# Summing the MLP's quarter products: additions by VectorE into SBUF, or accumulating DMAs into DRAM

## The chip, the cores and the metric

The kernel runs on one core of a Trainium2 chip. The metric is the device time of one execution in microseconds (us). Before the change the median of three runs is 1222.51 us.

The engines are named as the profile names them: PE is TensorE (matmuls; PEld are its weight loads), DVE is VectorE, ACT is ScalarE, POOL is GpSimd, SP is SyncE, which issues nearly all DMAs. SBUF is the on-chip memory of 128 partitions, PSUM the eight banks that matmuls write, DRAM the memory outside the core.

## The reference

One layer of a decoder trunk, for a prompt of 1024 tokens and a sample group of 8 x 8 tokens, in fp32, with a width of 1024. The change touches the MLP at the end of the layer alone:

```python
    h2 = rms_norm(x, norm2_g[l]) * (1.0 + scale2[:, None]) + shift2[:, None]
    ff = jnp.square(jax.nn.relu(h2 @ w_ff1[l])) @ w_ff2[l]
    x = x + gate2[:, None] * ff
```

`w_ff1` is 1024 x 4096 and `w_ff2` is 4096 x 1024. What comes before it (adaptive norm, one input projection, retention, windowed attention, two convolution modules, the output projection, a gated residual) gives `x`, the kernel's `x1`.

## The kernel before

All activations are held feature-major: 128 partitions by 8 feature blocks by 1088 tokens (1024 of the prompt and 64 of the sample). Every fp32 operand of a matmul is split into two parts, `hi` and `lo` (ACT rounds a copy, DVE subtracts it), and each product is three matmuls: hi by hi, hi by lo, lo by hi.

The MLP runs over 4096 hidden features in 8 groups (`NG`) of 4 blocks (`G`) of 128. For each group, `ff1_block` makes the hidden block from `h2`, for three chunks of tokens (384, 384 and 320 wide, `CH`), and `ff1_out` evicts it by ACT as Relu and Square. For `w_ff2`, a group's product is a product of 2 x 2 matrices of quarters: the group's weights and its hidden features are cut into quarters, and instead of eight quarter products seven are made, from sums and differences of quarters (Strassen's scheme in Winograd's form). The results go to four quarters of the output, named (i, j): i is the half of the 1024 output features (x1's blocks 4i to 4i + 3), j the half of the 1024 prompt tokens (512 columns, `H`).

The loop over g = 0 to 6 does one group's seven products, each in one call of `slot`, and between them the ff1 blocks of the next group (`ff1_items`, one or two blocks between two slots). In `slot`, for each of four output blocks m, `products` issues six matmuls of 128x512 into a PSUM bank (seven banks turn), and `add_to` adds the bank to every quarter of `x1` that needs it, by DVE; some products go to two quarters, so there are 40 such additions a group. The first group writes instead of adding. Quarter (1, 1) of `x1`, called `s22`, at the same time holds the sum that three of the four output quarters share. `x1` itself has been copied to DRAM before (`save`, `x1_save` in the profile, line 1407), so that its place is free for the sums.

The sample's 64 tokens go another way: `sample_parts` makes `st` (one ACT cast, one DVE subtraction), `sample_product` makes matmuls with it into a bank `sm`, and `sample_out` adds these into `acc`.

The eighth group is done in the plain way, four by four products with `products` over both halves of the features, 16 banks in the order (i, t) = (0, 0), (0, 1), (1, 0), (1, 1), four each. With it the output is finished: the old x1 is loaded from DRAM as `xr`, DVE adds `s22` to the two quarters that need it, then for every bank forms gate * sum + xr in place and adds gate * bank, and SP stores the result (line 1619).

PE, ACT and DVE keep the order of the program from `pinned[0] = True` on. The DMAs are not pinned: their order on a queue is chosen by the scheduler of the framework, by the times at which it takes them to be ready. Waits are put in by the framework from the overlaps of what is read and written, in SBUF and DRAM alike. `form` and `two` split an operand into its parts, `quarter` loads a quarter of `w_ff2` in SP's queue (line 1328), `loaded_weight` an ff1 block (line 1293).

All operations that go through the wrapper `InOrder` (ACT and DVE) carry its line in the profile, L158, and all matmuls L171; they are told apart by the names of their tiles.

Of the kernel before, what the change touches and what calls it, by code (L numbers as in the profile page):

```python
# [8 lines left out]
F32 = mybir.dt.float32  # L9
F32R = mybir.dt.float32r  # L10
AF = mybir.ActivationFunctionType
ALU = mybir.AluOpType
# [3 lines left out]
P = 128  # L16
D = 1024
NT = 1088
SEQ = 1024
# [121 lines left out]
def decoder_step(ctx: ExitStack, tc: tile.TileContext, A, O, where):  # L141
    nc = tc.nc
# [21 lines left out]
    ACT, DVE = InOrder(nc.scalar), InOrder(nc.vector)  # L164
# [44 lines left out]
    first = lambda n: view(cfirst, "cfirst", n)  # L209
# [119 lines left out]
    with ExitStack() as gctx:  # L329
# [765 lines left out]
        x = M[:, :, SEQ:]  # L1095
# [18 lines left out]
        def slot(c, i, evac, functions=None):  # L1114
            c0, w = CH[c]
            ps = mm_psum(w)
            product(ps, *ready[i], act_of(h, c), range(8))
            if i >= 4 or c == 2:
                tick()
            if functions:  # L1120
                table(functions)
            evac(IN_BLOCKS[i], c, c0, w, ps)
# [67 lines left out]
        for c, (c0, w) in enumerate(CH):  # L1190
            for j in range(2):
                ps = mm_psum(w)
# [9 lines left out]
            for j in range(2):  # L1202
                o, g = M[:, MA + j, c0 : c0 + w], gate[j][:, c0 : c0 + w]
# [7 lines left out]
    with ExitStack() as fctx:  # L1211
        xp = fctx.enter_context(tc.tile_pool(name="xp", bufs=1))
        x1 = xp.tile([P, 8, NT], F32, tag="x1", name="x1")
# [102 lines left out]

        NG = FF // P // G
        H = 512  # L1320
        RAW = ("w", "w", "ar", "ar")
# [73 lines left out]
        for c in range(3):  # L1395
            for b in range(G) if c < 2 else (2, 3, 0, 1):
                ps = mm_psum(CH[c][1])
# [10 lines left out]
                if c == 2 and b == 3:  # L1408
                    now_parts = two(a11, "ah", "al"), two(u.quarter(0, 0), "qh", "ql")
# [12 lines left out]
            parts = room(side + "h", F32R), room(side + "l", F32R)  # L1422
            return parts, cast(raw, *parts)

        def add_to(g, x, ps):

            i, j, m, minus, first = x
            dst = x1[:, 4 * i + m, H * j : H * j + H]
            if first and g == 0:
                if minus:  # L1430
                    DVE.tensor_scalar_mul(dst, ps, -1.0)
                else:
                    DVE.tensor_copy(dst, ps)
            else:
                DVE.tensor_tensor(out=dst, in0=dst, in1=ps, op=ALU.subtract if minus else ALU.add)

        def sample_parts(g, u):

# [30 lines left out]
        t = first_sum(u)  # L1469

        for g in range(NG - 1):
            nu = Group()
            state = {"f": 0}

            def ff1_items(n):
                for _ in range(n):
                    f = state["f"]
                    state["f"] += 1
                    b, c = f // 3, f % 3
                    x = G * (g + 1) + b  # L1480
                    ps = next_bank()[:, : CH[c][1]]
                    ff1_block(nu, x, c, ps)
                    ff1_out(nu, x, c, ps)
                    if c == 0:
                        ff1_split(x + 1)
                        ff1_load(x + 2)

            def slot(parts, targets, rests):

                rests = list(rests)  # L1490
                for m in range(4):
                    ps = next_bank()
                    products(ps, m, *parts, True, True)
                    if rests:
                        rests.pop(0)()
                    for i, j, minus, first in targets:
                        add_to(g, (i, j, m, minus, first), ps)


            DVE.tensor_tensor(out=s, in0=s, in1=a22, op=add)  # L1500
            w, r0 = form(s, "a")
            v, r1 = form(t, "q")
            parts2 = (w, v)
            slot(now_parts, [(0, 0, 0, 1), (1, 1, 0, 1)], [r0, r1])
            st = sample_parts(g, u)
            ff1_items(1)
            sm = sample_bank()
            sample_product(sm, st, now_parts[0], 0, True, False)
            ff1_items(1)


            DVE.tensor_tensor(out=s, in0=s, in1=a11, op=sub)
            DVE.tensor_tensor(out=t, in0=u.quarter(1, 1), in1=t, op=sub)
            w, r0 = form(s, "a")
            v, r1 = form(t, "q")
            parts3 = (w, v)
            slot(parts2, [(1, 1, 0, 0), (1, 0, 1, 1)], [r0, r1])
            a11 = quarter(g, 0, 0)
            ff1_items(2)


            DVE.tensor_tensor(out=t, in0=u.quarter(1, 0), in1=t, op=sub)
            w, r0 = form(a12, "a")
            v, r1 = form(u.quarter(1, 0), "q")
            parts4 = (w, v)
            slot(parts3, [(1, 1, 0, 0)], [r0, r1])
            ff1_items(2)


            t3 = u.quarter(0, 1)  # L1530
            DVE.tensor_tensor(out=t3, in0=u.quarter(1, 1), in1=t3, op=sub)
            DVE.tensor_tensor(out=s, in0=a12, in1=s, op=sub)
            w, r0 = form(s, "a")
            v, r1 = form(u.quarter(1, 1), "q")
            parts5 = (w, v)
            slot(parts4, [(0, 0, 0, 0)], [r0, r1])
            a21, a22 = quarter(g, 1, 0), quarter(g, 1, 1)
            sample_product(sm, st, parts4[0], 1, False, True)
            sample_out(g, 0, sm)
            ff1_items(1)  # L1540


            DVE.tensor_tensor(out=a11, in0=a11, in1=a21, op=sub)
            w, r0 = form(a11, "a")
            v, r1 = form(t3, "q")
            parts6 = (w, v)
            slot(parts5, [(0, 1, 0, 1)], [r0, r1])
            nxt = quarter(g + 1, 0, 0)
            ff1_items(2)


            w, r0 = form(a22, "a")
            v, r1 = form(t, "q")
            parts7 = (w, v)
            slot(parts6, [(1, 1, 0, 0), (0, 1, 1, 0)], [r0, r1])
            last = g + 1 == NG - 1
            s = quarter(g + 1, 0 if last else 1, 1 if last else 0)
            ff1_items(1)


            w, r0 = form(a21, "a")
            slot(parts7, [(1, 0, 0, 0)], [r0])
            sm = sample_bank()
            sample_product(sm, st, parts7[0], 1, True, False)
            sample_product(sm, st, w, 0, False, True)
            sample_out(g, 1, sm)
            if not last:
                a11 = nxt
                now_parts = two(a11, "ah", "al"), two(nu.quarter(0, 0), "qh", "ql")
                t = first_sum(nu)  # L1570
                a22, a12 = quarter(g + 1, 1, 1), quarter(g + 1, 0, 1)
                ff1_items(2)
            else:
                weights, parts = {(0, 0): two(nxt, "ah", "al")}, {(0, 0): two(nu.quarter(0, 0), "qh", "ql")}
                weights[0, 1] = two(s, "wh", "wl")
                ff1_items(1)
                parts[1, 0] = two(nu.quarter(1, 0), "q12", "t")
                ff1_items(1)
            u = nu


        g = NG - 1
        raw = [quarter(g, 1, j) for j in range(2)]
        xr = [hp.tile([P, 4, CH[0][1]], F32, tag=("hi0", "lo0", "hi1", "lo1")[m % 4], name=nm("xr")) for m in range(8)]
        xr = [x.rearrange("p a b -> p (a b)")[:, 0:SEQ] for x in xr]
        for m in range(8):
            nc.sync.dma_start(xr[m], save[:, m, :])
        s22 = x1[:, 4:8, H:SEQ]

        def sample_end(i):  # L1590

# [10 lines left out]
        for i in range(2):  # L1602
            for t in range(2):
                for m in range(4):
                    ps = next_bank()
                    for j in range(2):
                        products(ps, m, weights[i, j], parts[j, t], j == 0, j == 1)
                    if i == t == m == 0:
                        parts[0, 1] = two(u.quarter(0, 1), "qh", "ql")
                        parts[1, 1] = two(u.quarter(1, 1), "fr", "q11")  # L1610
                        st = sample_parts(g, u)
                    if (t, m) == (i, 0) and i == 0 or (t, m) == (1, 3) and i == 0:
                        x = x1[:, 0:4, H:SEQ] if m == 0 else x1[:, 4:8, 0:H]
                        DVE.tensor_tensor(out=x, in0=x, in1=s22, op=ALU.add)
                    x = x1[:, 4 * i + m, H * t : H * t + H]
                    gate = mod[:, 40 + 4 * i + m, 0:1]
                    DVE.scalar_tensor_tensor(x, x, gate, xr[4 * i + m][:, H * t : H * t + H], ALU.mult, ALU.add)
                    DVE.scalar_tensor_tensor(x, ps, gate, x, ALU.mult, ALU.add)
                    nc.sync.dma_start(O["yT"][:, 4 * i + m, H * t : H * t + H], x)
                    if i == 0 and t == 0 and m >= 2:  # L1620
                        weights[1, m - 2] = two(raw[m - 2], "ah", "al") if m == 3 else two(raw[0], "wh", "wl")
                    if t == 0 and m == 3:
                        sm = sample_bank()
                        for j in range(2):
                            sample_product(sm, st, weights[i, j], j, j == 0, j == 1)
                        sample_out(g, i, sm)
                    if t == 1 and m == 1:
                        sample_end(i)
# [74 lines left out]
```

## Time and profile before

| | |
|---|---|
| runs | 1222.51 us median, 1221.91 to 1224.81 |
| the profiled execution | 1222.88 us, its span 1220.8 us |
| granted TensorE clock | 0.999 |
| busy, share of the span | PE 99%, PEld 90%, DVE 66%, ACT 38%, POOL 1% |
| DMA | 113.72 MB, mean 93 GB/s |
| MLP loop, one group | 89.94 us |

A row of a timeline gives the start and the duration in us, the engine, the line, the operation, out<-in, and in square brackets how long the engine had been idle and what ended it. A row of a group gives the count, busy us, the mean in ns, and after the bar the idle time before. A row of waits gives who waited for whom: us in total, times, the longest. A row of DMA issues gives the queue's engine, the count, the size of one, and the median us from issue to landing. SPq is SP's queue.

### The profile page before, as it was taken

The numbers are of one execution on the slowest core, as the hardware profiler recorded it, in microseconds if no ns is written. First come the engines' busy times: TensorE is split into PE (matmuls) and PEld (weight loads), VectorE is DVE, ScalarE is ACT, GpSimd is POOL, SyncE is SP. The second block draws the span as 40 slices with busy tenths as digits, with TensorE's granted clock in tenths as the row PEclk, the third lists the DMA queues.
The fourth block names the chain that finished last, engine by engine and source line by source line (L and its number), as shares of the span: only waits on it lengthen the run. The fifth ranks groups of instructions, "written<-read, shape, count | busy, mean of one in ns | idle before, by whom it ended". The sixth has DMA issues, their size and how long they took to land.

```text
span 1220.8 us, 17251 instructions
## 1 busy us (share of the span) xinstructions
PE 1206.5 (99%) x7054; PEld 1095.5 (90%) x7054; DVE 809.7 (66%) x1288; ACT 465.0 (38%) x941; POOL 8.2 (1%) x28
## 2 busy tenths in 40 slices
PE   8999999999999999999999999999999999999998
PEld 6897789988899999989999999999999999999887
DVE  4789798884697538646566666666566566566575
ACT  4452333432367325633333334233333333333330
POOL 0000000000000000000000000000000000000000
PEclk9999999999999999999999999999999999999999
DMA  9748711120120813111211211221221121121332
GB/s 344 267 163 300 211 36 36 52 55 19 36 72 23 283 53 134 36 35 54 85 52 70 69 54 68 70 69 53 69 85 53 53 86 52 56 83 52 121 125 91
DMA packets 60165, 113.72 MB, mean 93 GB/s; under 512 B 13495, under 2 KB 29623, under 8 KB 60087
## 3 DMA queue, kind: packets, MB, share of 16 engines
q1 hardware_dynamic: 59943, 112.56, 27.9%
q8 instruction: 55, 0.90, 0.3%
q14 instruction: 23, 0.19, 0.1%
q10 hardware_dynamic: 144, 0.07, 0.0%
HBM read 101.90 MB, written 10.72 MB: 92 GB/s over the span
## 4 chain that ended last, share of the span: by engine, by line
PE 87%; DVE 8%; ACT 2%; SPq 1%; DMA 1%; issue 1%; DVEq 0%; ACTq 0%
PE ps L171 47%; PE mm L171 29%; PE pm L171 6%; DVE x L158 3%; PE sm L171 3%; PE pm L175 1%; PE ada L171 1%; DMA M<-in_xT 1%; SPq L391 1%; DVE al L158 1%; ACT ah L158 1%; DVE ql L158 1%; ACT q L158 0%; DVE qh L305 0%; DVE lo L312 0%
## 5 line engine op out<-in xcount | busy, mean ns | idle before, releaser
L171 PE MATMUL ps<-hi,wl 128*128 128x384 f32 (+1 forms) x672 | 219.9, 327 | 0.0
L171 PE MATMUL ps<-hi,wh 128*128 128x384 f32 (+1 forms) x672 | 219.7, 327 | 0.0
L171 PE MATMUL ps<-lo,wh 128*128 128x384 f32 (+1 forms) x672 | 219.4, 326 | 0.0
L171 PE MATMUL mm<-hi,wh 128*128 128x384 f32 (+1 forms) x544 | 181.8, 334 | 0.4 <-ACT hi L158 0.4
L171 PE MATMUL mm<-lo,wh 128*128 128x384 f32 (+1 forms) x544 | 178.0, 327 | 0.5 <-DVE lo L158 0.4
L171 PE MATMUL mm<-hi,wl 128*128 128x384 f32 (+1 forms) x544 | 177.5, 327 | 0.5 <-DVE wl L158 0.5
L158 ACT ACTIVATE q<-ps 128x384 f32<-128x384 f32 (+1 forms) x112 | 42.5, 380 | 351.8 <-PE ps L171 351.8
L158 DVE TENSOR_TENSOR x<-x,ps 128x512 f32<-128x512 f32 x264 | 165.3, 681 | 0.4 <-PE ps L171 0.4
L171 PE MATMUL ps<-qh,al 128*128 128x512 f32 x408 | 159.8, 392 | 0.0
L171 PE MATMUL ps<-qh,ah 128*128 128x512 f32 x408 | 159.2, 390 | 0.6 <-ACT us L1386 0.6
L171 PE MATMUL ps<-ql,ah 128*128 128x512 f32 x408 | 159.6, 391 | 0.0
L171 PEld LDWEIGHTS ps<-hi,wh 128*128 128x128 f32 x672 | 126.3, 188 | 2.2
L171 PEld LDWEIGHTS ps<-lo,wh 128*128 128x128 f32 x672 | 126.2, 188 | 2.2
L171 PEld LDWEIGHTS ps<-hi,wl 128*128 128x128 f32 x672 | 126.2, 188 | 0.0
L171 PEld LDWEIGHTS mm<-hi,wh 128*128 128x128 f32 x544 | 102.2, 188 | 8.9 <-issue 6.4
L171 PEld LDWEIGHTS mm<-lo,wh 128*128 128x128 f32 x544 | 102.3, 188 | 1.4 <-DVE lo L158 1.4
L171 PEld LDWEIGHTS mm<-hi,wl 128*128 128x128 f32 x544 | 102.1, 188 | 1.0 <-DVE wl L158 1.0
L158 DVE TENSOR_TENSOR wl<-fr,wh 128x1024 fp32r<-128x1024 f32 x27 | 33.1, 1226 | 102.4 <-ACT wh L158 102.4
L614 DVE SCALAR_TENSOR_TENSOR M<-glu,cmix,M 128x512 f32<-128x512 f32 (+2 forms) x150 | 97.8, 667 | 2.0
L171 PEld LDWEIGHTS ps<-qh,al 128*128 128x128 f32 x408 | 76.6, 188 | 16.1
L171 PEld LDWEIGHTS ps<-qh,ah 128*128 128x128 f32 x408 | 76.7, 188 | 15.4 <-ACT us L1386 0.9
L171 PEld LDWEIGHTS ps<-ql,ah 128*128 128x128 f32 x408 | 76.6, 188 | 14.7
(346 smaller groups left out, 1822.0 us busy)
## 6 DMA issues: line engine op xcount, KB each, us to landing
w<-in_w_ff SPq DMA_DIRECT2D x29, 512.0 KB, 3.6
ar<-in_w_ff SPq DMA_DIRECT2D x28, 512.0 KB, 3.7
fr<-in_w_ff SPq DMA_DIRECT2D x28, 512.0 KB, 3.6
w<-in_w_in SPq DMA_DIRECT2D x22, 512.0 KB, 5.0
M<-in_ada SPq DMA_DIRECT2D x20, 512.0 KB, 4.8
ada<-in_ada SPq DMA_DIRECT2D x16, 512.0 KB, 10.5
sw<-in_ada SPq DMA_DIRECT2D x9, 512.0 KB, 5.3
w<-in_w_out SPq DMA_DIRECT2D x8, 512.0 KB, 3.4
```

The lines of the kernel that those rows point to most:

```text
L158: i = f(*args, **kw)
L171: return tc.keep_in_program_order(nc.tensor.matmul(*args, **kw))
L175: return tc.keep_in_program_order(nc.tensor.transpose(*args, **kw))
L391: nc.sync.dma_start(t.rearrange("p (a k) -> p a k", a=4), src)
L614: DVE.scalar_tensor_tensor(dst, src(t), cdw[:, j, t : t + 1], dst, ALU.mult, ALU.add))))
```

## The change

The additions into `x1` by DVE are taken out of the loop. In their place ACT copies each bank of products out of PSUM into a stage, and two banks (one pair, 512 KB) are sent from POOL's queue by DMA into `kept`, a DRAM tensor with six sums: a plain DMA where a sum is written for the first time, an accumulating one (`accum_op=ALU.add`) afterwards. The stages are three of `x1`'s feature blocks (5, 6 and 7, their 1024 prompt columns), used in turn. `SUMS` names the sums to which each of the seven products goes: the first to two, the others to one each, so a group sends 16 such DMAs. The signs are no longer needed, as each sum holds one product or two with the same sign.

Ahead of the eighth group, `x1`'s four quarters are loaded from the sums that make them up: the first by a plain DMA of 1 MB on SP, the others by accumulating DMAs of 1 MB on POOL, ten in all. The two additions of `s22` by DVE are gone, since the shared sum is loaded into each quarter that needs it.

```diff
+        kept = nc.dram_tensor("y_parts", (P, 6, 4, H), F32, kind="Internal").ap()
+        SUMS = [(0, 1), (2,), (1,), (0,), (4,), (3,), (5,)]
+        started = set()
+        stage = [None]
-        def add_to(g, x, ps):
-            i, j, m, minus, first = x
-            dst = x1[:, 4 * i + m, H * j : H * j + H]
-            if first and g == 0:
-                if minus:
-                    DVE.tensor_scalar_mul(dst, ps, -1.0)
-                else:
-                    DVE.tensor_copy(dst, ps)
-            else:
-                DVE.tensor_tensor(out=dst, in0=dst, in1=ps, op=ALU.subtract if minus else ALU.add)
+        def add_to(g, n, m, ps):
+            if m % 2 == 0:
+                stage[0] = x1[:, 5 + stage[1] % 3, 0:1024]
+                stage[1] += 1
+            ACT.copy(stage[0][:, (m % 2) * H : (m % 2) * H + H], ps)
+            if m % 2:
+                src = stage[0].rearrange("p (m t) -> p m t", m=2)
+                for a in SUMS[n]:
+                    dst = kept[:, a, m - 1 : m + 1]
+                    if (a, m) in started:
+                        nc.gpsimd.dma_start(dst, src, accum_op=ALU.add)
+                    else:
+                        nc.gpsimd.dma_start(dst, src)
+                    started.add((a, m))
+        stage.append(0)
...
-                    for i, j, minus, first in targets:
-                        add_to(g, (i, j, m, minus, first), ps)
+                    add_to(g, n, m, ps)
...
-            slot(now_parts, [(0, 0, 0, 1), (1, 1, 0, 1)], [r0, r1])
+            slot(now_parts, 0, [r0, r1])
...
-        s22 = x1[:, 4:8, H:SEQ]
+        for i, j, terms in ((0, 0, (0,)), (0, 1, (1, 2, 4)), (1, 1, (1, 2, 3)), (1, 0, (1, 3, 5))):
+            for n, a in enumerate(terms):
+                dst = x1[:, 4 * i : 4 * i + 4, H * j : H * j + H]
+                if n:
+                    nc.gpsimd.dma_start(dst, kept[:, a], accum_op=ALU.add)
+                else:
+                    nc.sync.dma_start(dst, kept[:, a])
...
-                    if (t, m) == (i, 0) and i == 0 or (t, m) == (1, 3) and i == 0:
-                        x = x1[:, 0:4, H:SEQ] if m == 0 else x1[:, 4:8, 0:H]
-                        DVE.tensor_tensor(out=x, in0=x, in1=s22, op=ALU.add)
```

The other six calls of `slot` change in the same way, to the numbers 1 to 6.

More of the change, by code (lines that the diff above doesn't have):

```diff
@@ L1486, in ff1_items, with slot @@
                         ff1_load(x + 2)
-            def slot(parts, targets, rests):
+            def slot(parts, n, rests):
                 rests = list(rests)
@@ L1516, in decoder_step @@
             parts3 = (w, v)
-            slot(parts2, [(1, 1, 0, 0), (1, 0, 1, 1)], [r0, r1])
+            slot(parts2, 1, [r0, r1])
             a11 = quarter(g, 0, 0)
@@ L1525, in decoder_step @@
             parts4 = (w, v)
-            slot(parts3, [(1, 1, 0, 0)], [r0, r1])
+            slot(parts3, 2, [r0, r1])
             ff1_items(2)
@@ L1535, in decoder_step @@
             parts5 = (w, v)
-            slot(parts4, [(0, 0, 0, 0)], [r0, r1])
+            slot(parts4, 3, [r0, r1])
             a21, a22 = quarter(g, 1, 0), quarter(g, 1, 1)
@@ L1546, in decoder_step @@
             parts6 = (w, v)
-            slot(parts5, [(0, 1, 0, 1)], [r0, r1])
+            slot(parts5, 4, [r0, r1])
             nxt = quarter(g + 1, 0, 0)
@@ L1554, in decoder_step @@
             parts7 = (w, v)
-            slot(parts6, [(1, 1, 0, 0), (0, 1, 1, 0)], [r0, r1])
+            slot(parts6, 5, [r0, r1])
             last = g + 1 == NG - 1
@@ L1561, in decoder_step @@
             w, r0 = form(a21, "a")
-            slot(parts7, [(1, 0, 0, 0)], [r0])
+            slot(parts7, 6, [r0])
             sm = sample_bank()
```

## The prediction

> **What bounds the kernel now.** I read the page from the top: busy time, then the chain that ended last, and then left the page for the stretch that the change touches, one group of the MLP loop.
>
> ```profile
> PE 1206.5 (99%) x7054; PEld 1095.5 (90%) x7054; DVE 809.7 (66%) x1288; ACT 465.0 (38%) x941; POOL 8.2 (1%) x28
> PE 87%; DVE 8%; ACT 2%; SPq 1%; DMA 1%; issue 1%; DVEq 0%; ACTq 0%
> ```
>
> PE is the bound over the whole span. One group, from its first slot-1 matmul at 643.29 to the same one a group later, by windows (columns: length, PE, PEld, DVE, ACT, POOL busy, PEclk, DMA share, GB/s), and what PE waited for from 530 us to the end:
>
> ```profile
> 643.29:733.23 89.94, 89.73 (x473) 82.03 (x473) 57.00 (x71) 32.34 (x60) 0.00 (x0) 1.00 0.19 65
> PE sm L171 <- DVE st L158: 2.6, 7, 1.4
> PE ps L171 <- ACT us L1386: 0.6, 1, 0.6
> ```
>
> A group lasts 89.94 us and PE works in 89.73 of them at full clock. In the 690 us from 530 on PE idles 3.2 us in all, and 2.6 of these are one wait, met once in each of seven groups: the sample product's `st`. So the change can gain some 3 us there at most, and can lose as much as new waits make. The chain names DVE for 8%, but most of that runs beside a busy PE.
>
> **The `st` wait, which the change touches.** Slot 0 of the next group, on PE, ACT and DVE:
>
> ```profile
> 718.02 0.39 PE L171 MATMUL ps<-qh,ah 128*128 128x512 f32 x1
> 723.49 0.33 PE L171 MATMUL ps<-hi,wh 128*128 128x384 f32 x1
> 727.50 0.34 PE L171 MATMUL ps<-hi,wl 128*128 128x384 f32 x1
> 728.05 0.47 PE L171 MATMUL sm<-ah,st 128*128 128x512 f32 x1 [0.21 <-DVE st L158]
> ...
> 720.30 1.05 ACT L158 CAST qh<-t 128x1024 fp32r<-128x1024 f32 x1
> 721.25 0.40 ACT L158 CAST st<-us 128x256 fp32r<-128x256 f32 x1
> ...
> 723.89 3.67 DVE L158 TENSOR_TENSOR x<-x,ps 128x512 f32<-128x512 f32 x6
> 727.48 0.42 DVE L158 TENSOR_TENSOR st<-us,st 128x256 fp32r<-128x256 f32 x1
> ```
>
> The four products of slot 0 take 718.02 to 723.49, so 1.37 us each. DVE's second part of `st` stands behind eight additions into x1 and ends at 727.90, and PE, free at 727.7, starts `sm` at 728.05. After the change the additions are gone from DVE, but ACT's part of `st` now stands behind four copies. Price of a copy of 128x512 out of PSUM: ACT's reads of PSUM in this group, and DVE's addition for comparison:
>
> ```profile
> L158 ACT ACTIVATE q<-ps 128x256 f32<-128x256 f32 x8 | 3.0, 375 | 12.3 <-PE ps L171 12.3
> L158 ACT ACTIVATE q<-ps 128x384 f32<-128x384 f32 x4 | 2.0, 492 | 23.1 <-PE ps L171 23.1
> L158 DVE TENSOR_TENSOR x<-x,ps 128x512 f32<-128x512 f32 x41 | 25.7, 681 | 0.0
> ```
>
> 128 columns more cost 117 ns, so 512 cost about 0.61 us (a different function on the same path; I take it as an estimate). ACT's cast ends at 721.35; its four copies end near 722.0, 722.6, 723.2 and, behind the fourth product at 723.6, 724.3; `st` on ACT ends at 724.7 and on DVE at 725.1, 2.6 us ahead of PE. The wait goes in all seven groups: minus 2.6 us.
>
> **ACT and DVE.** 28 copies a group by 0.61 us are 17 us more on ACT: 32.3 becomes 49.4 of 89.9. In one slot ACT has two casts (2.1 us) and four copies (2.4 us) within 5.5 us, and mostly two ff1 blocks of 4 us (723.49 to 727.7) lie before the next slot, so PSUM banks come free sooner than now. DVE loses 40 additions, 25 of its 57 us (the 41st row is the window's edge). Neither is on the path: nothing. What it costs if a copy has to wait is below, since behind it on ACT stand the Relus, the squares and the casts that PE needs.
>
> **PE's pace beside ACT.** Slot 1 in two halves of twelve matmuls:
>
> ```profile
> 643.29 0.39 PE L171 MATMUL ps<-qh,ah 128*128 128x512 f32 x1
> 646.05 0.39 PE L171 MATMUL ps<-qh,ah 128*128 128x512 f32 x1
> 648.77 0.31 PE L171 MATMUL ps<-hi,wh 128*128 128x320 f32 x1
> ```
>
> The first half, beside ACT's casts, takes 2.76 us, the second, beside DVE's additions, 2.72. If ACT's copies slow the second half likewise, 49 slots cost 49 x 0.04 = 2.0 us; if they don't, nothing. I take 1.0, the middle, for no row tells the two apart.
>
> **The accumulating DMAs, the term that decides.** Each group issues 8 targets by 2 pairs = 16 transfers of 512 KB from POOL (in the first group 12 of them plain). The trace has none that adds. The nearest rows are the plain ones, by queue and landing in the same group, and the copies of x1 to DRAM:
>
> ```profile
> q1 hardware_dynamic: 2480, 5.77, 19.1%
> fr<-in_w_ff SPq DMA_DIRECT2D x4, 512.0 KB, 3.5
> w<-in_w_ff SPq DMA_DIRECT2D x4, 512.0 KB, 3.7
> ar<-in_w_ff SPq DMA_DIRECT2D x3, 512.0 KB, 3.7
> ...
> x_save<-x SPq DMA_DIRECT2D x2, 1536.0 KB, 6.4
> x_save<-x SPq DMA_DIRECT2D x1, 1024.0 KB, 5.1
> ```
>
> Eleven loads take 19.1% of 89.94 = 17.2 us of all 16 engines: 1.56 us each. From 1024 to 1536 KB landing grows by 1.3 us: 2.6 us for 1 MB on top of a fixed 2.5. An addition reads two operands and writes one. Lower end: no dearer than plain, 1.56 us. Upper end: nothing overlaps, a transfer reads like a load that lands in 3.7 us and then writes back like another, 7.4. I take 2 times plain, 3.12 us, nearer the lower end, as only the reading doubles and the plain row is that of many transfers that overlap. Then a group needs 16 x 3.12 + 17.2 = 67 us of engine time in 90: it fits, and PE does not see it. It stops fitting at (89.94 - 17.2) / 16 = 4.55 us, 2.9 times plain. The Trainium skill, "Collectives: The Full Stack", section "The bandwidth ceiling: the fold count and why AG ≠ RS ≠ AR", says that a DMA addition is bound by its two reads and runs at about half the rate of a copy (62.28 against 32.35 GB/s); by that estimate a transfer is 1.93 x 1.56 = 3.0 us and a group 65 us. No row here shows an addition yet.
>
> Three stages turn: the copies of a pair wait for the pair three before it. The tightest place by order is pair 4 on pair 1. Slot 0's first pair is out at 722.6; slot 1 starts at 733.2 (643.29 + 89.94), slot 2 some 5.5 + 8 later, its first copy near 748: four transfers have 25 us, less 2.5 to land, 5.7 each. So the mean rate of 4.55 binds first. The weight loads share the engines; at half of them each, 1.56 becomes 3.1 and they land near 5.3 instead of 3.7. Their cover:
>
> ```profile
> 668.04 0.37 SPq L1328 DMA_DIRECT2D ar<-in_w_ff  x1
> ...
> 683.55 1.22 DVE L158 TENSOR_TENSOR ar<-ar,w 128x1024 f32<-128x1024 f32 x1
> ```
>
> One of the shortest waits 15.5 us between issue and use: nothing. If that cover goes, PE waits for the casts of the next slot.
>
> **The end.** x1 has to come back: four plain loads of 1 MB on SP, six accumulating ones on POOL, before the last 16 products' results can be gated.
>
> ```profile
> 1150.64 3.05 SPq L1587 DMA_DIRECT2D xr<-x_save  x4
> 1156.18 0.38 SPq L1328 DMA_DIRECT2D ar<-in_w_ff  x1
> ...
> 1158.39 0.69 DVE L158 TENSOR_TENSOR x<-x,ps 128x512 f32<-128x512 f32 x1 [0.44 <-PE ps L171]
> 1174.92 0.74 DVE L158 SCALAR_TENSOR_TENSOR x<-x,mod,xr 128x512 f32<-128x512 f32 x1
> 1175.77 0.75 DVE L158 SCALAR_TENSOR_TENSOR x<-ps,mod,x 128x512 f32<-128x512 f32 x1
> 1176.43 0.75 DVE L158 SCALAR_TENSOR_TENSOR x<-x,mod,xr 128x512 f32<-128x512 f32 x1
> 1205.13 0.69 DVE L158 TENSOR_TENSOR acc<-sm,acc 128x512 f32<-128x512 f32 x1 [1.06 <-PE sm L171]
> 1211.41 0.42 DVE L158 TENSOR_TENSOR q<-ps,mod 128x256 f32<-128x256 f32 x1
> 1216.95 0.75 DVE L158 SCALAR_TENSOR_TENSOR x<-ps,mod,x 128x512 f32<-128x512 f32 x1 [1.31 <-PE ps L171]
> ```
>
> The DMA order is the scheduler's (xr goes ahead of the weight quarter that the code loads first), so the upper half's loads (i = 0), whose place is free and whose sums end early, should go out in time. The lower half's overlap the stages: they wait for the last pair. Its copies end near 1159, its transfers at 1159 + 3.1 + 2.5 = 1164.7; a 1 MB load lands 5.1 later, 1169.8. An added 1 MB at 2 times takes 2.5 + 5.2 = 7.7; four, one behind the other, end at 1200.6. DVE must then gate eight results at 1.51 us (1174.92 to 1176.43) and do the sample's 0.69 and twice 0.42: 13.6 us. It is done now at 1217.7, so 1204.1 is early enough: 3.5 us to spare, and nothing is lost. At 3 times they take 10.3 each and end at 1212.5: 8.4 us lost. The two 128x2048 additions that DVE loses here are beside PE: nothing.
>
> **Sum.** 1222.88 (the profiled execution, of which the span is 1220.8) - 2.6 + 1.0 = 1221.3; the median of the runs shown is 0.4 below that execution, so 1221. Less than 0.3% (3.7 us) is what a measurement of this kernel can't tell from no change, so this is "no change".
>
> **Rivals.**
>
> *The additions fill the DMA engines* (slower). From 4.55 us a transfer on, six groups each grow by 16 X + 17.2 - 89.9: the stage isn't free, ACT's copy waits, behind it the Relus and casts, then PE. At 3 times (4.68): 2.2 x 6 = 13, with 8 at the end, 1243. The same comes about if the transfers don't overlap, each paying its fixed part: 16 x (2.5 + 3.1) = 90, just a group, and at the upper end 16 x 7.4 = 118, 28 x 6 = 171 more, 1392. Against such queueing:
>
> ```profile
> 1176.55 10.77 SPq L1619 DMA_DIRECT2D out_yT<-x  x6
> 1187.81 0.38 SPq L1600 DMA_DIRECT2D out_yT<-x  x1
> out_yT<-x SPq DMA_DIRECT2D x16, 256.0 KB, 2.0
> ```
>
> The store at 1187.81 is issued 0.5 us after the issue of another into another part of the same DRAM tensor ends (1187.32), under the 2.0 to landing: such writes don't wait for each other. For it: nothing here shows POOL issuing a DMA at all. 24%.
>
> *Only the end is late* (slower). The loop fits, but the chains load, add, add are a microsecond or two longer than I made them, or POOL and SP issue them late. From 1204.1 on every microsecond counts: 4 to 15 us, say 1230. The Trainium skill, "DMA: Bandwidth & Descriptors", section "Rules for kernel authors", says that an accumulating DMA must wait for an earlier one on the same bytes to land. By that rule each link pays its landing, as I counted it; no row here shows two on the same bytes. 17%.
>
> *A real gain.* If PE's pace doesn't suffer and the first group's start gains too, 1218 or less, over 0.3%: little else idles. 5%.
>
> **How the numbers follow.** No change 54%, its own range 1218 to 1226; end late 17%; engines full 24%, half of that beyond 1275. Faster 0.05, same 0.54, slower 0.41. Range 1218 to 1275 (53 / 6 + 72.7 = 16 X at X near 5.1, 3.3 times plain): it leaves out 5% below and some 12% above.
>
> **What will show it.** Right: a group still 90 us, `st` gone from PE's waits, ACT near 49 us and DVE near 32 in a group, DMA share near 0.75, additions landing 5 to 8 us after issue. Wrong: ACT's copies waiting for a DMA, a share near 1, PE idle inside the groups; or DVE waiting for x1 after 1195 with the loop unchanged.

## The result

The changed kernel takes 1232.59 us (median, 1232.46 to 1234.23) against 1222.21 before: a ratio of 1.0083, 95% interval 1.0066 to 1.0101, so 10.4 us slower where no change was forecast. The MLP loop became faster, by 4.6 us. The end lost 14.5.

### The profile page after: what moved, and what is told of

Read it like the earlier page. It is cut to its first block, busy times and chain, and to the rows that moved or that the text cites. A ratio compares the mean times of both kernels' runs of the same rounds, so it can differ in the third digit from the quotient of the medians.

```text
span 1230.6 us, 17492 instructions
## 1 busy us (share of the span) xinstructions
PE 1211.3 (98%) x7054; PEld 1099.4 (89%) x7054; DVE 639.4 (52%) x1006; ACT 566.8 (46%) x1137; POOL 107.8 (9%) x146
## 4 chain that ended last, share of the span: by engine, by line
PE 86%; DMA 4%; DVE 4%; issue 3%; SPq 1%; ACT 1%; POOL 1%; DVEq 0%; POOLq 0%; ACTq 0%
PE ps L171 47%; PE mm L171 29%; PE pm L171 6%; PE sm L171 2%; DMA x<-y_parts 2%; DMA y_parts<-x 2%; PE pm L175 1%; PE ada L171 1%; DMA M<-in_xT 1%; SPq L391 1%; DVE x L158 0%; DVE qh L305 0%; DVE lo L312 0%; DVE ql L305 0%; DVE M L614 0%
## 5 line engine op out<-in xcount | busy, mean ns | idle before, releaser
L1442 POOL DMA_DIRECT2D y_parts<-x x100 | 86.5, 933 | 462.0 <-ACT x L158 460.3
L158 ACT COPY x<-ps 128x512 f32<-128x512 f32 x196 | 106.5, 585 | 38.2 <-PE ps L171 26.1
## 6 DMA issues: line engine op xcount, KB each, us to landing
ada<-in_ada SPq DMA_DIRECT2D x16, 512.0 KB, 10.5
```

The costliest lines, as they stand in the source:

```text
L158: i = f(*args, **kw)
L1442: nc.gpsimd.dma_start(dst, src, accum_op=ALU.add)
```

## The profile after

The profiled execution's span is 1230.6 us (before 1220.8). Its page: busy time, the chain, and the issues of the new transfers (size of one, median us from issue to landing).

```profile
PE 1211.3 (98%) x7054; PEld 1099.4 (89%) x7054; DVE 639.4 (52%) x1006; ACT 566.8 (46%) x1137; POOL 107.8 (9%) x146
PE 86%; DMA 4%; DVE 4%; issue 3%; SPq 1%; ACT 1%; POOL 1%; DVEq 0%; POOLq 0%; ACTq 0%
y_parts<-x POOLq DMA_DIRECT2D x112, 512.0 KB, 7.2
x<-y_parts POOLq DMA_DIRECT2D x6, 1024.0 KB, 12.4
```

DMA, hardly in the chain before, now has 4% of it. The time is not lost in the loop: one group by windows, and ninety microseconds with the later groups' DMA share (columns as in the prediction: length, PE, PEld, DVE, ACT, POOL, PEclk, DMA share, GB/s).

```profile
589.62:679.08 89.46, 89.46 (x473) 82.03 (x472) 32.67 (x29) 47.40 (x90) 11.77 (x16) 1.00 0.63 159
```

```profile
650.00:740.00 90.00, 90.00 (x477) 82.56 (x476) 33.27 (x30) 47.24 (x89) 13.61 (x16) 1.00 0.76 159
```

A group takes 89.46 us instead of 89.94 and PE has no idle time in it. When slot 6 of the last loop group has ended and its `sm` begins, the changed kernel is ahead: 1153.58 on its timeline, 1158.19 before. This matmul and the last one, first in the changed kernel, then before:

```profile
1153.58 0.39 PE L171 MATMUL sm<-ah,st 128*128 128x512 f32 x1
1226.44 0.39 PE L171 MATMUL ps<-fr,al 128*128 128x512 f32 x1
```

```profile
1158.19 0.39 PE L171 MATMUL sm<-ah,st 128*128 128x512 f32 x1
1216.53 0.39 PE L171 MATMUL ps<-fr,al 128*128 128x512 f32 x1
```

From there to the last matmul (1226.44 now, 1216.53 before) it takes 72.9 us instead of 58.3: 14.5 lost. The waits of PE from 530 us on (without one of 0.6 us at the start of the loop, which is there before too), and those of DVE and ACT on a DMA from 1150 us on:

```profile
PE ps L171 <- DVE acc L158: 4.5, 1, 4.5
PE ps L171 <- ACT qh L158: 2.1, 1, 2.1
PE ps L171 <- DVE ql L158: 1.0, 1, 1.0
...
DVE x L158 <- DMA x<-y_parts: 15.1, 1, 15.1
ACT x L158 <- DMA y_parts<-x: 10.7, 1, 10.7
```

The clock (the last column but two) in stretches of 5 us:

```profile
1165.00:1170.00 5.00, 3.64 (x8) 2.23 (x9) 4.16 (x4) 4.87 (x12) 0.00 (x0) 0.59 1.06 270
1220.00:1225.00 5.00, 5.00 (x15) 3.92 (x15) 2.25 (x5) 0.00 (x0) 0.00 (x0) 0.61 0.28 81
```

There are two stalls. In the first, ACT waits 10.7 us for a stage, with the casts of the next operands behind the copy, and PE idles 3.1 us. In the second, DVE waits 15.1 us for x1's quarter (1, 0), with `sample_out` and so `acc` behind it; PE, which comes to the small matmuls of `sample_end` two products later, idles 4.5. That makes 7.6 us; the other 6.9 are, by difference, PE's restarts and its clock, which stands at 0.59 to 0.73 after both stalls. The first, on PE:

```profile
1165.40 0.49 PE L171 MATMUL ps<-qh,ah 128*128 128x512 f32 x1 [2.15 <-ACT qh L158]
1166.85 0.80 PE L171 MATMUL ps<-ql,ah 128*128 128x512 f32 x1 [0.95 <-DVE ql L158]
...
1167.87 0.63 PE L171 MATMUL ps<-qh,ah 128*128 128x512 f32 x1
1168.30 0.63 PE L171 MATMUL ps<-ql,ah 128*128 128x512 f32 x1
...
1172.82 0.39 PE L171 MATMUL ps<-qh,al 128*128 128x512 f32 x1
1173.05 0.39 PE L171 MATMUL ps<-qh,ah 128*128 128x512 f32 x1
```

Matmuls start 0.43 us apart until 1172.5, then 0.23 again. The roots of both stalls stand in POOL's queue, in one issue on SP's, and in ACT's copies into the stages:

```profile
1141.67 1.67 ACT L158 COPY x<-ps 128x512 f32<-128x512 f32 x3
1145.13 1.29 POOL L1603 DMA_DIRECT2D x<-y_parts  x1 [10.17 <-issue]
1145.90 2.30 POOL L1442 DMA_DIRECT2D y_parts<-x  x2
1162.38 1.07 ACT L158 COPY x<-ps 128x512 f32<-128x512 f32 x2 [10.74 <-DMA y_parts<-x]
1163.75 0.84 POOL L1442 DMA_DIRECT2D y_parts<-x  x1 [10.36 <-ACT x L158]
1174.11 0.92 SPq L1605 DMA_DIRECT2D x<-y_parts  x2
1180.38 1.30 POOL L1603 DMA_DIRECT2D x<-y_parts  x1 [15.79 <-DVE wl L158]
1184.02 1.30 POOL L1603 DMA_DIRECT2D x<-y_parts  x1 [2.34 <-DMA x<-y_parts]
1191.86 1.28 POOL L1603 DMA_DIRECT2D x<-y_parts  x1 [6.55 <-DMA x<-y_parts]
1198.41 1.27 POOL L1603 DMA_DIRECT2D x<-y_parts  x1 [5.26 <-DMA x<-y_parts]
1210.21 0.75 DVE L158 SCALAR_TENSOR_TENSOR x<-x,mod,xr 128x512 f32<-128x512 f32 x1 [15.07 <-DMA x<-y_parts]
```

One of the upper half's two accumulating loads (1145.13) goes out after POOL has stood for 10 us, and two transfers of pairs followed it at 1145.90; the copies of the first of these two pairs are the first two of the three in the row at 1141.67 and had ended near 1142.8. The last pair of all needs the stage of that pair, the third before it, so ACT stood until that pair's transfer had landed, 16.5 us after the issue. Of ACT's 10.7 us some 3 are thus the time that the transfer was held on POOL's queue; the rest is its slow landing. The last pair's went at 1163.75, the lower half's plain loads only at 1174.11, and the four adding ones, two at a time, ended at 1210.2. (The addition at 1180.38 needs nothing of DVE, which is named as its releaser; what it needs is the plain load, so I read that load as landed then.)

## The experiments

Two theories of the end stand against each other. *Full engines*: what has to be moved after 1110 us, 4 MB plain, 6 MB adding at twice the cost and 4 MB of the old x1, fills the DMA engines (share 0.85 to 1.13 from 1125 to 1210 us). *Order*: POOL's queue stands still behind loads that wait for a landing, and the pairs behind them. st_early and four_sums have five runs each, the other experiments one.

**st_early: the loop's gain without any of the change.** Kernel before:

```diff
-            slot(now_parts, [(0, 0, 0, 1), (1, 1, 0, 1)], [r0, r1])
             st = sample_parts(g, u)
+            slot(now_parts, [(0, 0, 0, 1), (1, 1, 0, 1)], [r0, r1])
```

> The kernel before, with the sample's st made ahead of slot 0's additions instead of behind them; nothing else changed. Theory A (the whole lead that the changed kernel has when the tail begins, 4.6 us, comes from the st wait: 2.6 us idle and the rest PE's restart after it): 1222.2 - 4.6 = 1217.6, no st wait left, groups of 89.5 us. Theory B (only the idle time counts, the rest of the lead comes from DVE leaving PSUM alone): 1219.6, groups of 89.7 us.

1217.55 us, a ratio of 0.9962 to the kernel before (0.9948 to 0.9975). One group by windows, and then all of PE's waits from 530 us on:

```profile
641.30:730.76 89.46, 89.46 (x473) 82.02 (x472) 56.97 (x71) 32.36 (x61) 0.00 (x0) 1.00 0.20 65
```

```profile
PE ps L171 <- ACT us L1386: 0.6, 1, 0.6
```

The same 89.46 as the changed kernel, with DVE as busy as ever. Theory A holds: a wait listed with 0.21 us idle costs 0.48 a group (89.94 less 89.46) with PE's restart, and nothing of the lead came from taking the additions off DVE.

**small_adds: the bytes of the six adding loads.** Changed kernel, each of the six on 64 of 512 columns:

```diff
-                    nc.gpsimd.dma_start(dst, kept[:, a], accum_op=ALU.add)
+                    nc.gpsimd.dma_start(dst[:, :, 0:64], kept[:, a, :, 0:64], accum_op=ALU.add)
```

> The changed kernel; the six accumulating loads into x1 at the end keep their place, order and waits but move 64 of 512 columns, so the output lacks most of the shared sums. Theory 'full engines' (both stalls at the end come from the bytes that the DMA engines have to move after 1110 us): ACT's wait of 10.7 us for a stage and DVE's of 15.1 us for x1 both go, PE is not idle after 1110, span 1216 to 1217. Theory 'order' (POOL's queue stands still behind each load that must land first, and the pairs' transfers behind it): ACT's wait stays above 5 us, PE idles 2 us or more near 1163, span above 1220.

1218.74 us, span 1217.0. ACT's and DVE's waits on a DMA after 1100 us:

```profile
ACT x L158 <- DMA y_parts<-x: 7.1, 1, 7.1
DVE x L158 <- DMA x<-y_parts: 4.5, 1, 4.5
```

The span is that of "full engines", but neither wait is gone, as that theory had it, and the stage wait of 7.1 us is that of "order": it stays, and PE's cover is just long enough (1.1 us idle). The loss of the end goes with these bytes; the stage wait does not go with them alone.

**pairs_first: the order alone.** Changed kernel, `tc.keep_in_program_order(...)` around the six adding loads, which puts them behind the last pair.

> The changed kernel with the six accumulating loads held behind the last pair's transfer on POOL's queue. The bytes are the same, only the order changes. 'Order': the stage wait of 10.7 us goes, PE does not idle near 1163, and the span falls to 1224 or less. 'Full engines': the stage wait falls too (6.4 us less work ahead of the pairs), but the same work stands later, all six behind each other: x1's last quarter comes back after 1210, DVE waits 15 us or more, and the span is 1228 to 1236.

1239.04 us, span 1237.3, which neither theory had ("order" 1224 or less, "full engines" 1228 to 1236). ACT no longer waits for a stage, and PE does not idle near 1163 though the engines are full:

```profile
1150.00:1180.00 30.00, 30.00 (x147) 26.12 (x147) 17.59 (x20) 12.49 (x21) 4.77 (x5) 1.00 1.05 318
```

But now the six come behind the last pair:

```profile
DVE x L158 <- DMA x<-y_parts: 31.0, 2, 22.6
PE ps L171 <- DVE acc L158: 18.8, 1, 18.8
```

Both theories let the stage wait fall here, so that alone does not tell them apart. The share of 1.05 does (0.94 to 1.09 in the changed kernel's windows of these 30 us): full engines made no first stall where no load stands ahead of the pairs, as the one at 1145 does in the changed kernel. The second stall grows with the amount of work behind the last pair. Mending the one by order makes the other worse.

**few_xr: other bytes in the same stretch.** Changed kernel: two of the eight loads of the old x1, used for all eight.

> The changed kernel; two of the eight loads of the old x1 are made and their content stands for all eight, so the output is not the reference's. 3 MB less move between 1146 and 1165 us. 'Full engines': 9 us less work there, ACT's wait for a stage falls from 10.7 to below 4 us, PE does not idle near 1163, the lower half's chain starts some 7 us earlier and x1 is back near 1203: span 1217 to 1220. 'Order' (POOL's queue): the wait for a stage stays near 10 and the span near 1228.

1222.25 us, span 1220.1. ACT still waits 7.7 us for the stage, a miss of "full engines" (below 4); PE idles 1.3 us there and 2.2 at `acc`; DVE waits 12.8 us for x1. 3 MB less, 9 us of the engines at 1.56 for 512 KB, shorten the span by 10.5 us, to the upper edge of what "full engines" said. So bytes count in the first stall as well as order: with the order kept, fewer bytes leave 7.1 or 7.7 us of the wait, which PE nearly covers.

**late_end: what PE waits for in the second stall.** Changed kernel:

```diff
-                    if t == 1 and m == 1:
+                    if t == 1 and m == (3 if i else 1):
```

> The changed kernel with sample_end(1) behind the last product instead of two products earlier. If the second PE stall (4.5 us) is its small matmuls waiting for acc behind DVE's late gating: PE no longer waits for acc, the clock stays full after 1205, DVE still waits about 15 us for x1 and then gates eight results and the sample in 13.6 us from 1210: span about 1227. If PE would have waited for PSUM banks anyway: a wait for a bank in its place and a span of 1229 to 1231.

1227.89 us, span 1226.0. DVE waits as before (16.9 us), PE only 0.9 for `acc`, and for no bank. The wait was `sample_end`, not a lack of PSUM banks. Of the 4.6 us that the span is shorter, 0.7 are x1's quarter, which is back at 1209.5 instead of 1210.2; the rest, about 3.9, goes with the wait.

**ladder: the clock.** Kernel before, `sample_parts`:

```diff
+            for _ in range((1, 3, 5, 7, 9, 12, 16, 1)[g]):
                 DVE.tensor_tensor(out=st[:, :, 64:P], in0=u.sample, in1=st[:, :, 0:64], op=ALU.subtract)
```

> The kernel before; DVE repeats its st subtraction 1, 3, 5, 7, 9, 12 and 16 times in the groups 0 to 6, so that PE waits in the middle of the loop for about 1.4, 0.9, 1.6, 2.2, 2.9, 3.9 and 5.3 us, with no more DMA than before. If PE's clock falls after a wait (the changed kernel shows 0.6 after waits of 3.1 and 4.5 us): matmuls 0.43 us apart for some 7 us after the longer waits, about 3 us lost besides each, and none after the short ones; 1244 to 1250. If the low clock there came from the DMA load and not from the wait: 0.23 us apart all through, 1238.

1247.86 us. Two of the waits, on PE:

```profile
822.51 0.47 PE L171 MATMUL sm<-ah,st 128*128 128x512 f32 x1 [2.97 <-DVE st L158]
823.05 0.39 PE L171 MATMUL sm<-ah,st 128*128 128x512 f32 x1
823.27 0.39 PE L171 MATMUL sm<-al,st 128*128 128x512 f32 x1
...
916.12 0.47 PE L171 MATMUL sm<-ah,st 128*128 128x512 f32 x1 [3.89 <-DVE st L158]
917.26 0.52 PE L171 MATMUL ps<-hi,wh 128*128 128x384 f32 x1
917.58 0.52 PE L171 MATMUL ps<-lo,wh 128*128 128x384 f32 x1
```

After 2.97 us idle the pace is full (0.23 for 512 columns), after 3.89 it falls to 0.32 for 384, without any additional DMA, and so it does after the two longer waits, 5.27 and 7.11. So a wait can make it without the transfers. The slow stretch lasted 3 to 4 us here and cost 1.5 to 1.8, against 7 us and some 3.4 after each stall of the changed kernel: that difference is open. What starts it is not the length of one wait alone. In the changed kernel's first stall two waits do, 2.15 and 0.95 us with one matmul between, and in late_end's 0.66 and 0.95 us (before the matmuls at 1163.92 and 1165.37): its matmuls are then 0.43 us apart until 1168.3. In few_xr three waits in the same place, 0.31, 0.25 and 0.76, leave the pace full. The Trainium skill, "TensorE: Matmul & The Clock Gate", section "What's actually happening", has the clock at half after an idle window of about 3.4 us and full again after as long a busy one: the ladder agrees with both, the wait (2.97 no, 3.89 yes) and the length; the shorter waits in late_end and the 7 us of the changed kernel do not.

**double_adds: the price of an addition in the loop.** Changed kernel, each transfer of groups 0 to 5 made once more into another DRAM tensor:

```diff
+                    if 0 <= g <= 5:
+                        nc.gpsimd.dma_start(again[:, a, m - 1 : m + 1], src, ...)
```

> The changed kernel; in the groups 0 to 5 each transfer into the six sums is made a second time, into another DRAM tensor that nothing reads (plain in group 0, adding in 1 to 5): 32 a group. If an addition of 512 KB takes 3.2 us of all engines, as the busy share of the changed kernel's loop says: 32 x 3.2 + 17.2 = 119.6 us a group where it adds, DMA share near 1, some 150 us more in all. If they cost only what a plain transfer does (1.6): 68 us, hidden, the span near 1231. If they don't overlap (7.2 each, the time to landing): 230 us a group.

1256.08 us. One group, from an ff1 cast to the same cast of the next:

```profile
920.16:1016.06 95.90, 91.85 (x474) 83.35 (x473) 33.37 (x30) 46.13 (x89) 27.02 (x34) 0.98 1.06 238
```

The engines are full and a group takes 95.9 us: with the 17.2 us of the weight loads as in the prediction, (95.9 - 17.2) / 32 = 2.46 us for 512 KB, not 3.2. The busy share of the changed kernel's loop (0.76) overstates it, presumably as packets of several transfers wait side by side. None of the three numbers expected came out; the first theory's mechanism did.

**add_price: an addition alone.** Kernel before, six transfers on POOL, each on the bytes of the one ahead, while little else moves:

```diff
+        nc.gpsimd.dma_start(there, old)
+        nc.gpsimd.dma_start(there, old, accum_op=ALU.add)
+        nc.gpsimd.dma_start(there[:, 0, 0:128], old[:, 0, 0:128], accum_op=ALU.add)
...
```

> The kernel before; while the DMA engines are quiet (500 to 540 us) POOL issues six transfers, each on the bytes of the one ahead of it and so behind its landing: a quarter of the old x1 from DRAM back into its own place (1 MB, plain), added once (1 MB) and once in part (64 KB); then from there to a scratch in DRAM the same three. x1's place is written anew afterwards, so the output stays the reference's. If an addition's landing is a fixed part like a plain one's plus its engine time (2.5 + 4.9 for 1 MB by the doubled loop), and the 11.5 to 14 us at the end come from sharing the engines: 1 MB lands 7 to 8 us after issue, 64 KB under 3.5. If an addition has a longer fixed part (about 5): 1 MB 9.5 to 10.5, 64 KB 5 or more, and the plain 1 MB about 5 to 6 in both cases.

```profile
506.02 0.94 POOL L1412 DMA_DIRECT2D x<-x_save  x1 [263.86 <-ACT ql L307]
512.23 1.29 POOL L1413 DMA_DIRECT2D x<-x_save  x1 [5.26 <-DMA x<-x_save]
521.56 0.86 POOL L1414 DMA_DIRECT2D x<-x_save  x1 [8.04 <-DMA x<-x_save]
524.44 0.76 POOL L1415 DMA_DIRECT2D scratch<-x  x1 [2.01 <-DMA x<-x_save]
529.31 1.21 POOL L1416 DMA_DIRECT2D scratch<-x  x1 [4.11 <-DMA scratch<-x]
538.40 0.88 POOL L1417 DMA_DIRECT2D scratch<-x  x1 [7.88 <-DMA scratch<-x]
```

Each issue follows the landing of the one before: 1 MB plain 6.2 and 4.9 us, adding 9.3 and 9.1; 64 KB adding 2.9. A long fixed part is not there; 1 MB alone takes somewhat more than the 7 to 8 expected, and I put the 11.5 to 14.4 at the end of the changed kernel down to two of them sharing the engines with each other and the stores, which no run here separates.

**four_sums: the end without adding loads.** Changed kernel with four sums, two of them taken from the shared one by DVE at the end:

```diff
-        SUMS = [(0, 1), (2,), (1,), (0,), (4,), (3,), (5,)]
+        SUMS = [(0, 1), (1, 3), (1,), (0,), (2,), (1, 2), (3,)]
-            ACT.copy(...)
+            ACT.activation(..., ps, AF.Identity, scale=-1.0 if n in (4, 6) else 1.0)
-((0, 0, (0,)), (0, 1, (1, 2, 4)), (1, 1, (1, 2, 3)), (1, 0, (1, 3, 5)))
+((0, 0, (0,)), (0, 1, (2,)), (1, 1, (1,)), (1, 0, (3,)))
+                        DVE.tensor_tensor(out=x, in0=x1[:, 4:8, H:SEQ], in1=x, op=ALU.subtract)
```

> The changed kernel with four sums in place of six (the shared sum, and two that are subtracted from it at the end by DVE; ACT writes two of the seven products with the sign turned): 20 transfers of 512 KB a group instead of 16, and at the end four plain loads of 1 MB and no accumulating one. If the end's loss lies in the bytes of the six accumulating loads and an addition of 512 KB takes 3.2 us of the engines (81 of 89.5 us a group): no PE wait of 3 us or more, 1217 to 1219. If 0.9 of the engines is too much for transfers that come in bursts (eight in the first two slots): ACT waits for stages inside the groups, PE with it, 1222 or more.

1218.28 us, 0.9963 (0.995 to 0.9977) of the kernel before. The loop, and the stretch of the changed kernel's first stall:

```profile
560.00:1100.00 540.00, 540.00 (x2853) 495.43 (x2852) 198.62 (x178) 284.53 (x534) 102.77 (x120) 1.00 0.83 182
1150.00:1180.00 30.00, 30.00 (x147) 26.12 (x147) 17.38 (x20) 13.22 (x22) 1.70 (x2) 1.00 1.04 327
```

20 transfers a group are hidden as the 16 were, PE is never idle, and the end loses nothing: again full engines near 1163 and no stall, with no load on POOL's queue. It is better than the changed kernel and no better than st_early, which moves one line.

## Why the prediction was wrong

*Right.* The additions are hidden in the loop: DMA share 0.76 (forecast near 0.75), landing 7.2 us (5 to 8), ACT 47.4 us a group (49.4), DVE 32.7 (32), the `st` wait gone. The forecast factor of 2 lies between what was measured: 1.6 times a plain transfer in full engines (2.46 to 1.56), about 2.4 times alone (9.2 against 5.6 us, each less the 2.9 of a small one). So the agreement of the share is one of busy shares alone: a transfer was put at 3.12 us of the engines and took 2.46 by the length of double_adds' group.

*Mis-sized in the loop.* The `st` wait was taken at 2.6 us; it cost 4.6 with PE's restarts (st_early). The 1.0 for PE's pace beside ACT was nothing.

*Wrong: the end.* The step that failed is "3.5 us to spare". Its four links in a row were 30.8 us and took 29.8 (1180.4 to 1210.2), which is luck: they were four of 7.7 us, one behind the other, and came out as two side by side, twice, of 11.5 to 14.4 (one alone takes 9.2). What made the chain late is where it begins, at 1180.4 and not 1169.8. "Its copies end near 1159" became 1163.4, its transfer landed after 10.4 us instead of 5.6, and the plain load after 6.3 instead of 5.1. The first took the stage as free, the other two the price of quiet engines. The upper half's four loads, which were to "go out in time", and xr were costed at nothing, though they stand on the same engines and two of them, the adding ones, on POOL ahead of pairs (pairs_first, small_adds, few_xr).

The wait for a stage was looked for in one place alone, and misread there: pair 4 is slot 1's second pair and not slot 2's first, so it comes some 15 us behind the pair whose stage it needs, not 25 (from near 1078 to near 1093 in the changed kernel's last loop group). In the loop no copy waited even so. At the end there are only 9 us, from 1142.8 to 1151.6, where ACT begins to wait.

*Left out.* The end was counted on DVE alone; by that count x1's return at 1210.2 instead of 1204.1 costs 6.1 us. PE waits for `acc` at `sample_end`, behind DVE's late gating (late_end), and such a wait costs the clock too (ladder): of 14.5 us lost, 7.6 are idle and 6.9 restarts and slow matmuls.

The rival "only the end is late", at 17% and 1230, is what happened. That the engines are full was right for the last 100 us, not for the loop.

## What to carry to other kernels

Where a bound engine has a short wait once per round, look for the instruction in front of the one that it waits for: here, moving one line gave all that the large change gained in the loop. Work that is taken off an engine with time to spare into the DMA queues has to be loaded back, and here the price of the way back was that of the busiest stretch, not of a quiet one; count every transfer of that stretch on its engines, and on its queue what stands behind each that waits. Two stalls of PE, 7.6 us in all, cost nearly twice their length here.

## What the runs showed of the hardware

An accumulating DMA of 64 KB lands in 2.9 us (add_price), hardly more than the 2.5 that the prediction worked out as the fixed part of plain ones, and one of 512 KB takes 2.46 us of full engines (double_adds). A listed wait of 0.21 us on PE cost 0.48 (st_early). PE's clock halved after single waits of 3.89 us and more, not after 2.97 (ladder), but also after two of 0.66 and 0.95 us with one matmul between (late_end); how long it then stays low, 3 us or 7, differed. Both are open.
